# Hybrid attention and retention layer: program order for the first four gate products, and later stores of scaled attention pieces

## The chip, the cores and the metric

One core of one Trainium2 chip runs the whole layer in one launch. The metric is the device time of that launch in microseconds, the median of several executions. Lower is better. Engines are named as in the profile: PE is TensorE's matmul, PEld its weight load, DVE is VectorE, ACT is ScalarE, POOL is GpSimd, SP is SyncE, which here only issues DMAs.

## The reference

One layer over 1024 latent tokens of width 1024, with 256 context tokens as a prefix. After a modulated RMSNorm one projection feeds neighbourhood attention, bidirectional retention and two merge gates. The part that this case touches:

```
(xq, xk, xv, xrq, xrk, xrv, xrg, xga, xgb) = split(hx @ w_in)
o_na  = neighbourhood_attention(xq, xk, xv, context keys)
o_ret = norm(bi_retention(xrq, xrk, xrv)) * silu(xrg)
merged = sigmoid(xga) * (o_na @ w_proj_na) + sigmoid(xgb) * (o_ret @ w_proj_ret)
x = x + g1 * (merged @ w_out)
x = x + g2 * conv_ffn(modulate(rmsnorm(x)))
```

All of it is in float32. The output is a final RMSNorm of `x`.

## The kernel before, in words

**Arithmetic.** A float32 product is made of three matmuls on split operands: high times high, high times low, low times high. `split` (L88, L89) makes the halves: ScalarE casts a tile to its high half (L88), VectorE subtracts it from the source to get the low half (L89). Weight tiles in split form are `wc` (six buffers, shared by all stages); as they come from memory they are `raw` (three buffers) or, in the gate stage, `wr` (ten buffers).

**Stages, in order of time.** Start and norm, attention, retention (four heads, some 390 to 720 us), the projection of attention (`pn`), the gate products (class `Gates`, some 770 to 930 us), the projection of retention with the merge (`pr`), the output projection (`om`), the conv FFN (`u` again, with another class on the same base `Seven`), and its down projection (`y`).

**The gate products.** `Seven` makes a product of 2 by 2 blocks with seven block products in place of eight. For one gate, a11, a12, a21 and a22 are blocks of the weights and B11 to B22 blocks of the activations. s1 to s4 are sums of weight blocks (L1423 to L1426, on POOL, but for the first gate, where VectorE makes s1 to s3), T1 to T4 are sums of activations made earlier (`hx_sums`, tiles `hxT`). `step(n)` issues block product n, 12 matmuls at L1409 into one of three PSUM banks X, Y, Z (`u`):

- step 0: a11 times B11 into X; ScalarE copies X to p1 (`pu`, L1449)
- step 1: s2 times T2 into Y; VectorE makes u2 = Y + p1 (`pu`, L1452)
- step 2: s1 times T1 into Z
- step 3: s3 times T3 on top of Y; VectorE makes u3 = Y + p1 (`pu`, L1458), and the first result block
- steps 4 to 6: a12 on top of X, a22 on top of Y, s4 on top of Z; three more result blocks

Step 3 writes the bank that u2 reads, so it follows u2. `interleaved` overlaps the gates: the second gate's step 0 comes behind the first gate's step 3, then the two alternate. In program order that is gate and step (0,0), (0,1), (0,2), (0,3), (1,0), (0,4), (1,1), (0,5), (1,2), (0,6), (1,3). Each `prod` splits its own weights right before its matmuls, except the first gate's a11, which `wload` splits during the `pn` stage (`first`).

**What sets the order.** The kernel is written in program order, and a scheduler of the framework then orders the instructions of each engine. An instruction wrapped in `late` (L533) keeps its place in program order on its engine. Each engine, and SP's queue of DMA issues, runs strictly in the order that results; a waiting instruction holds up all behind it.

**The scaled pieces.** `scaled` (L1265) runs during retention, one step per call of `next(rows)`. Each of 32 steps loads a 128 by 128 piece of attention sums (`os`, from `d_sum`) and the matching reciprocals (`or`, from `d_rec`), multiplies on VectorE (L1283, pinned with `late`), and stores the piece to `d_on` (L1274). The load runs one step ahead; the store is issued one step behind its multiply; both tiles have three buffers. All these DMAs are issued on SP, in one queue with the retention weights (`raw`, L93), the stores and loads of `down_sums` (`d_w`, `pj`), and others. The retention weights end in tiles `wc` or, for the last two of a head, `wx`.

Of the kernel before, what the change touches and what calls it, by code (L numbers as in the profile page):

```python
# [8 lines left out]
F32 = mybir.dt.float32  # L9
F32R = mybir.dt.float32r  # L10
AF = mybir.ActivationFunctionType
ALU = mybir.AluOpType
# [4 lines left out]
P = 128  # L17
D = 1024
KB = D // P
# [21 lines left out]
def tile_hybrid_layer(ctx, tc: tile.TileContext, io, dbg=None):  # L41
    nc = tc.nc
    vec, act, pool, pe, sync = nc.vector, nc.scalar, nc.gpsimd, nc.tensor, nc.sync
# [43 lines left out]
    def split(hi, lo, src, lo_eng=None):  # L87
        act.copy(hi, src)  # L88
        (lo_eng or vec).tensor_tensor(lo, src, hi.bitcast(F32), ALU.subtract)  # L89
# [221 lines left out]
    first = [[wtile() for _ in range(2)] for _ in range(3)]  # L311
# [221 lines left out]
    late = tc.keep_in_program_order  # L533
# [47 lines left out]
    nraw, nxt = {}, {}  # L581
# [472 lines left out]
    rt = sb("ret", "right")  # L1054
# [209 lines left out]

    def scaled():  # L1265
        def load(pr, j):
            o, r = (rt.tile([P, P], F32, tag=t, bufs=3, name=t) for t in ("os", "or"))
            sync.dma_start(o, d_sum[pr, :, j])
            src = d_rec[2 * pr : 2 * pr + 2, j * P : (j + 1) * P].unsqueeze(1).to_broadcast([2, HD, P])
            sync.dma_start(r, src)  # L1270
            return o, r

        def store(pr, j, o):
            sync.dma_start(d_on[pr, :, :, j].rearrange("h p q -> p h q"), o.rearrange("p (h q) -> p h q", h=2))  # L1274

        steps = [(pr, j) for pr in range(NPAIR) for j in range(NJ)]
        nxt, done = load(*steps[0]), None
        yield
        for n, at in enumerate(steps):
            o, r = nxt  # L1280
            if n + 1 < len(steps):
                nxt = load(*steps[n + 1])
            late(vec.tensor_tensor(o, o, r, ALU.mult))  # L1283
            if done:
                store(*done)
            done = (*at, o)
            yield
        store(*done)

    rows = scaled()  # L1290

# [30 lines left out]
    mix, last = None, (None, None)  # L1322
    for h in range(RH):
        head = Head(h)
        for i in range(NCB + NTB):
# [3 lines left out]
            last = (head, i)  # L1329
# [38 lines left out]
    def g_ps(name):  # L1368
        return pg.tile([P, 512], F32, tag="g", bufs=6, name=name)
# [44 lines left out]
        tc.add_manual_dep(ins.ins, prev.name, mybir.DependencyInfo(mybir.DependencyClass.Sync, mybir.DependencyReason.DATA))  # L1414

    class Seven:
        loaded, first = False, None

        def load(self, pin=lambda ins: ins, eng=None):
            self.loaded, own, eng = True, late if eng else lambda ins: ins, eng or pool  # L1420
# [7 lines left out]
        def fetch(self, b, half):  # L1428
            pass

        def prod(self, bank, a, c, first, last, w=None):
            if w is None:
                w = wtile()
                split(w[:, 0], w[:, 1], a)
            for k, (xh, xl) in enumerate(self.moving(c)):
                open3(bank, w[:, 0, k * P : (k + 1) * P], w[:, 1, k * P : (k + 1) * P], xh, xl, first and k == 0, last and k == KH - 1)

# [4 lines left out]
        def step(self, n):  # L1442
            if n == 0:
                if not self.loaded:
                    self.load()
                self.banks()
                self.p1, self.u2, self.u3 = (self.tmp() for _ in range(3))
                self.prod(self.X, self.a11, "B11", True, False, self.first)
                act.copy(self.p1, self.X)  # L1449
            elif n == 1:  # L1450
                self.prod(self.Y, self.s2, "T2", True, False)
                vec.tensor_tensor(self.u2, self.Y, self.p1, ALU.add)  # L1452
            elif n == 2:
                self.prod(self.Z, self.s1, "T1", True, False)
            elif n == 3:
                self.fetch(1, 1)
                self.prod(self.Y, self.s3, "T3", False, False)
                vec.tensor_tensor(self.u3, self.Y, self.p1, ALU.add)  # L1458
                self.add(1, 1, self.Z, self.u3)
            elif n == 4:  # L1460
                self.fetch(0, 0)
                self.prod(self.X, self.a12, "B21", False, True)
                self.c11()
            elif n == 5:
                self.fetch(1, 0)
                self.prod(self.Y, self.a22, "T4", False, True)
                self.add(1, 0, self.Y, self.p1)
            else:
                self.fetch(0, 1)
                self.prod(self.Z, self.s4, "B22", False, True)  # L1470
                self.add(0, 1, self.Z, self.u2)

    HALVES = {"B11": (0, 0), "B21": (KH, 0), "B22": (KH, 1)}
# [4 lines left out]
    class Gates(Seven):  # L1478


        def __init__(self, kind, n):
            self.kind, self.n = kind, n
            w = io["w_rg" if kind == "ret" else "w_gate"]
            self.src = {(b, i): w[n, b, i] for b in range(2) for i in range(2)}
            self.c = {}
# [42 lines left out]
    for db in range(KB):  # L1528
        if db + 2 < KB:
            wp[db + 2] = [wload(io["w_pna"][db + 2, 0])]  # L1530
        if db in HX_SUMS:
            hs = hx_sums(HX_SUMS.index(db))
            next(hs)
        for half in range(2):
            sl_ = slice(half * 512, half * 512 + 512)
            m = g_ps("pn")
            mm_a(m, wp[db], lambda k: ona[0][:, k, sl_], lambda k: ona[1][:, k, sl_])
            t = onap.tile([P, 512], F32, tag="pn", bufs=3, name="pnt")
            if (db, 0) in spilled:
                g = onap.tile([P, 512], F32, tag="sg", bufs=2, name="sgt")  # L1540
                sync.dma_start(g, d_gate[2 * db, half])
                act.activation(g, g, AF.Sigmoid)
                vec.tensor_tensor(t, m, g, ALU.mult)
            else:
                act.copy(t, m)
            act.dma_start(d_pn[db, half], t)
        if db == HX_SUMS[-1]:
            gu[0].first = wload(gu[0].src[0, 0])
            gu[0].load(late, vec)
        if db in HX_SUMS:  # L1550
            next(hs)
# [24 lines left out]
    steps = interleaved(0, len(gu))  # L1576
    n0, fetched, wp0 = steps.index((len(gu) - 1, 0)), None, []
    fetches = {d: (k // 8, k % 8) for k, d in enumerate((-6, -5, -4, -3, 1, 2, 3, 4, 7, 9))}
    for n, (i, k) in enumerate(steps):
        gu[i].step(k)  # L1580
        if n % 3 == 1:
            next(gate_sums, None)
        if fetched:
            split(*fetched[0], fetched[1])
            fetched = None
        if n - n0 in fetches:
            fetched = orr_raw(*fetches[n - n0])
        if n >= len(steps) - 3 and len(wp0) < 2:
            wp0.append(wload(io["w_pret"][0, len(wp0)]))
# [237 lines left out]
    class Up(Seven):  # L1827


        def __init__(self, n, j):  # L1830
            self.n, self.j = n, j
            self.src = {(b, i): io["w_up"][j, b, i] for b in range(2) for i in range(2)}

        def raw(self, src):
# [293 lines left out]
```

## Time and profile before

| what | before |
|---|---|
| median of 3 runs | 1764.5 us (1763.49 to 1765.6) |
| profiled execution: device time | 1764.47 us |
| profiled execution: span in the trace | 1762.7 us |
| mean granted TensorE clock | 0.992 |
| instructions | 24593 |
| moved by DMA | 268.20 MB, mean 152 GB/s |

In the rows below a number pair at the start is start and length in us from the span's start, then engine, line, operation, output and input tiles, shape, and how many in a row; a bracket at the end is idle time just before, with what ended it. `ACTq` and `SPq` are DMA issues on those engines' queues. The rows of the stretches give busy time and instruction counts of PE, PEld, DVE, ACT and POOL, then the granted TensorE clock (1.00 is full), the busy share of the DMA engines and GB/s. The rows of waits give total us, times and the longest.

### The profile page before, as it was taken

Reading aid. Unit: us, or ns where it says so; the run is one execution under the profiler, and the core shown is the slowest. Engines: PE = TensorE matmul, PEld = TensorE weight load, DVE = VectorE, ACT = ScalarE, POOL = GpSimd, SP = SyncE. Lnnn points to the kernel's source line nnn. Section 1 sums busy time; section 2 is a strip of 40 time slices with the busy share of each in tenths; the row PEclk is TensorE's granted clock in tenths of the full one; section 3 lists DMA queues with packets and bytes.
Section 4 is the critical chain, followed back from the end, with each engine's and each line's share of the span. In section 5 each row is a group of like instructions: output and inputs, shape, how many; then the busy total and the mean of one; then the engine's idle time right before and its main releaser. Section 6 shows DMA issues by size and latency. Waiting matters only on the chain.

```text
span 1762.7 us, 24593 instructions
## 1 busy us (share of the span) xinstructions
PE 1715.2 (97%) x8262; PEld 1415.7 (80%) x8262; DVE 1317.0 (75%) x2509; ACT 848.1 (48%) x1802; POOL 550.6 (31%) x458
## 2 busy tenths in 40 slices
PE   8799999999999999999999999999999999999997
PEld 3588888888788888878888888888888888888886
DVE  5978888765687777777665556888899899876655
ACT  5666666652443434543444333544444444554444
POOL 2610000002233343136422400265555555111444
PEclk9899999999999999999999999999999999999998
DMA  9134334533333312567659643733323332586754
GB/s 348 52 116 135 105 113 120 154 127 105 94 111 87 109 57 77 188 218 246 209 176 314 227 144 130 259 127 111 99 90 99 118 113 90 179 287 193 244 167 150
DMA packets 157247, 268.20 MB, mean 152 GB/s; under 512 B 25184, under 2 KB 45888, under 8 KB 157120
## 3 DMA queue, kind: packets, MB, share of 16 engines
q1 hardware_dynamic: 139200, 245.65, 42.9%
q10 hardware_dynamic: 17920, 20.98, 3.3%
q8 instruction: 65, 1.06, 0.3%
q14 instruction: 62, 0.51, 0.1%
HBM read 192.32 MB, written 71.61 MB: 150 GB/s over the span
## 4 chain that ended last, share of the span: by engine, by line
PE 45%; issue 5%; DVE 3%; POOL 3%; ACT 1%; DMA 0%; POOLq 0%; ACTq 0%; DVEq 0%
PE u L1409 27%; PE y L1409 4%; PE om L123 2%; PE om L124 2%; PE om L125 2%; PE pr L113 2%; PE pr L112 2%; PE pr L114 2%; DVE wc L89 1%; PE u L113 1%; PE u L114 1%; PE u L112 1%; POOL x L1942 1%; PE pn L113 0%; PE pn L112 0%
## 5 line engine op out<-in xcount | busy, mean ns | idle before, releaser
L1409 PE MATMUL u<-T,wc 128*128 128x512 f32 x960 | 225.5, 390 | 0.3 <-ACT pu L1449 0.2
L1409 PE MATMUL y<-wc,ahl 128*128 128x512 f32 x924 | 212.2, 391 | 2.3 <-DVE wc L89 1.8
L1409 PEld LDWEIGHTS u<-T,wc 128*128 128x128 f32 x960 | 179.4, 188 | 40.9 <-ACT pu L1449 3.6
L1409 PEld LDWEIGHTS y<-wc,ahl 128*128 128x128 f32 x924 | 174.4, 189 | 39.8 <-DVE wc L89 2.5
L89 DVE TENSOR_TENSOR wc<-ur,wc 128x512 fp32r<-128x512 f32 x137 | 126.2, 923 | 62.3 <-ACT wc L88 62.3
L88 ACT CAST wc<-ur 128x512 fp32r<-128x512 f32 x137 | 85.1, 622 | 125.1 <-PE y L1409 72.6
L113 PE MATMUL mm<-low,wc 128*128 128x512 f32 (+1 forms) x328 | 124.4, 379 | 0.0
L1409 PE MATMUL u<-h2a,wc 128*128 128x512 f32 x480 | 112.5, 390 | 0.7 <-DVE pu L1458 0.7
L112 PE MATMUL mm<-hx,wc 128*128 128x512 f32 x264 | 106.9, 405 | 0.3 <-DVE vc L223 0.3
L1409 PEld LDWEIGHTS u<-h2a,wc 128*128 128x128 f32 x480 | 89.9, 188 | 20.1 <-DVE pu L1458 1.1
L114 PE MATMUL mm<-hx,wc 128*128 128x512 f32 x264 | 105.9, 401 | 0.0
L1409 PE MATMUL u<-hxT,wc 128*128 128x512 f32 x384 | 92.5, 397 | 3.9 <-DVE pu L1452 3.9
L88 ACT CAST wc<-s 128x512 fp32r<-128x512 f32 x80 | 49.6, 621 | 90.2 <-PE u L1409 87.0
L125 PE MATMUL mm<-wc,low 128*128 128x512 f32 (+1 forms) x240 | 91.4, 381 | 0.0
L1409 PEld LDWEIGHTS u<-hxT,wc 128*128 128x128 f32 x384 | 73.5, 192 | 19.9 <-issue 4.3
L89 DVE TENSOR_TENSOR wc<-s,wc 128x512 fp32r<-128x512 f32 x80 | 85.8, 1072 | 3.1 <-ACT wc L88 2.6
L1552 POOL TENSOR_TENSOR col<-col,bcol 128x32 f32<-128x32 f32 x1 | 0.2, 250 | 278.4 <-DVE st L482 278.4
L88 ACT CAST wc<-raw 128x512 fp32r<-128x512 f32 x93 | 57.3, 620 | 47.8 <-DMA raw<-in_w_ret 7.1
L89 DVE TENSOR_TENSOR wc<-raw,wc 128x512 fp32r<-128x512 f32 x93 | 63.3, 689 | 18.6 <-ACT wc L88 18.2
L123 PE MATMUL mm<-wc,hx 128*128 128x512 f32 x192 | 75.2, 392 | 0.6 <-ACT r L1111 0.6
L124 PE MATMUL mm<-wc,hx 128*128 128x512 f32 x192 | 75.2, 392 | 0.0
L89 DVE TENSOR_TENSOR wc<-wr,wc 128x512 fp32r<-128x512 f32 x55 | 53.4, 976 | 18.2 <-ACT wc L88 17.5
(396 smaller groups left out, 4663.1 us busy)
## 6 DMA issues: line engine op xcount, KB each, us to landing
ur<-in_w_up SPq DMA_DIRECT2D x80, 256.0 KB
ur<-d_a SPq DMA_DIRECT2D x77, 256.0 KB
aw<-in_w_ada SPq DMA_DIRECT2D x32, 512.0 KB
pj<-in_w_down SPq DMA_DIRECT2D x44, 256.0 KB
d_w<-pj SPq DMA_DIRECT2D x44, 256.0 KB
d_a<-sa SPq DMA_DIRECT2D x44, 256.0 KB
ur<-d_w SPq DMA_DIRECT2D x44, 256.0 KB
d_a<-at SPq DMA_DIRECT2D x33, 256.0 KB
```

Of the source, the lines that this page charges most:

```text
L88: act.copy(hi, src)
L89: (lo_eng or vec).tensor_tensor(lo, src, hi.bitcast(F32), ALU.subtract)
L112: pe.matmul(out, wh, xh, start=k == 0, stop=False)
L113: pe.matmul(out, wh, xl, start=False, stop=False)
L114: pe.matmul(out, wl, xh, start=False, stop=k == n - 1)
L123: pe.matmul(out, ah, bh, start=first, stop=False)
L124: pe.matmul(out, ah, bl, start=False, stop=False)
L125: pe.matmul(out, al, bh, start=False, stop=last)
L1409: pe.matmul(out, a, b, start=first and n == 0, stop=last and n == 2, skip_group_check=True)
L1552: pool.tensor_tensor(col[:, 16:48], col[:, 16:48], bcol[:, 16:48], ALU.add)
L1942: pool.tensor_tensor(z, z, fg[:, gs(dh)], ALU.mult)
```

## The change

Four edits, none of which adds or removes arithmetic.

1. The weight split of `Seven` becomes a method `split(n)`, kept by the number of the step in a table `w`; `prod` splits only what is not in the table. The first gate's s2 and s1 are split during the `pn` stage, in front of its last half, and pinned there. s3 of the first gate is split behind step 0, a11 of the second gate behind step 1 (which also loads the second gate there), a12 of the first gate behind step 2, all pinned.
2. In the first four products, the copy p1 (ScalarE), u2 and u3 (VectorE) are pinned too.
3. In `scaled`, the store is issued two steps behind its multiply.
4. In `scaled`, `os` has four buffers and `or` two.

```diff
@@ scaled
-            o, r = (rt.tile([P, P], F32, tag=t, bufs=3, name=t) for t in ("os", "or"))
+            o, r = (rt.tile([P, P], F32, tag=t, bufs=n, name=t) for t, n in (("os", 4), ("or", 2)))
...
             late(vec.tensor_tensor(o, o, r, ALU.mult))
-            if done:
-                store(*done)
-            done = (*at, o)
+            done.append((*at, o))
+            if n > 1:
+                store(*done.pop(0))
             yield
-        store(*done)
+        for d in done:
+            store(*d)
@@ Seven
-        loaded, first = False, None
+        loaded, pin = False, staticmethod(lambda ins: ins)
...
-        def prod(self, bank, a, c, first, last, w=None):
-            if w is None:
-                w = wtile()
-                split(w[:, 0], w[:, 1], a)
+        def split(self, n, pin=lambda ins: ins):
+            a = (self.a11, self.s2, self.s1, self.s3, self.a12, self.a22, self.s4)[n]
+            self.w[n] = w = wtile()
+            pin(act.copy(w[:, 0], a))
+            pin(vec.tensor_tensor(w[:, 1], a, w[:, 0].bitcast(F32), ALU.subtract))
+
+        def prod(self, bank, n, c, first, last):
+            if n not in self.w:
+                self.split(n)
+            w = self.w.pop(n)
...
-                act.copy(self.p1, self.X)
+                self.pin(act.copy(self.p1, self.X))
...
-                vec.tensor_tensor(self.u2, self.Y, self.p1, ALU.add)
+                self.pin(vec.tensor_tensor(self.u2, self.Y, self.p1, ALU.add))
...
-                vec.tensor_tensor(self.u3, self.Y, self.p1, ALU.add)
+                self.pin(vec.tensor_tensor(self.u3, self.Y, self.p1, ALU.add))
@@ pn stage, ahead of each half of a block
+            if (db, half) == (KB - 1, 1):
+                for n in (1, 2):
+                    gu[0].split(n, late)
...
-            gu[0].first = wload(gu[0].src[0, 0])
+            gu[0].w[0] = wload(gu[0].src[0, 0])
@@ gate stage
+    ahead = {0: (0, 3), 1: (1, 0), 2: (0, 4)}
     for n, (i, k) in enumerate(steps):
+        gu[i].pin = late if n < 4 else lambda ins: ins
         gu[i].step(k)
+        if n in ahead:
+            j, k = ahead[n]
+            if not gu[j].loaded:
+                gu[j].load()
+            gu[j].split(k, late)
```

What becomes of it on the engines, at three places. PE and POOL have the same order before and after.

ScalarE, at the end of the `pn` stage and the start of the gates, before. `wr_8924`, `wr_8923` and `wr_8925` are the first gate's s2, s1 and s3, `wr_8921` its a12, `wr_9070` and `wr_9075` the second gate's a11 and s2, and `pu_8988` is p1:

```order
L88 CAST wc_9004<-wr_8924 128x512
L88 CAST wc_9028<-wr_8923 128x512
L1545 COPY pnt_8968<-pn_8955 128x512
L1559 COPY arow_8977<-tpa_8975 32x128
L1546 DMA d_pn_64<-pnt_8968 128x512
L88 CAST wc_9045<-wr_8925 128x512
L88 CAST wc_9088<-wr_9070 128x512
L1449 COPY pu_8988<-u_8985 128x512
L88 CAST wc_9109<-wr_8921 128x512
L88 CAST wc_9128<-wr_9075 128x512
```

The same place with the change, where the lines are those of the new file, `wr_9030` and `wr_9035` are the second gate's a11 and s2, and `pu_8994` is p1:

```order
L1435 CAST wc_8955<-wr_8924 128x512
L1435 CAST wc_8958<-wr_8923 128x512
L1555 COPY pnt_8974<-pn_8961 128x512
L1569 COPY arow_8983<-tpa_8981 32x128
L1556 DMA d_pn_64<-pnt_8974 128x512
L1456 COPY pu_8994<-u_8991 128x512
L1435 CAST wc_9010<-wr_8925 128x512
L1435 CAST wc_9042<-wr_9030 128x512
L1435 CAST wc_9065<-wr_8921 128x512
L1435 CAST wc_9128<-wr_9035 128x512
```

p1 has moved ahead of the casts of s3 and of the second gate's a11; the rest stands as it did.

VectorE at the same time, before; `pu_8989` is u2 and `pu_8990` is u3, `wr_8917` is the first gate's a22 and `wr_9074` the second gate's s1:

```order
L89 TENSOR_TENSOR wc_9004<-wr_8924,wc_9004 128x512
L89 TENSOR_TENSOR wc_9028<-wr_8923,wc_9028 128x512
L89 TENSOR_TENSOR wc_9045<-wr_8925,wc_9045 128x512
L89 TENSOR_TENSOR wc_9088<-wr_9070,wc_9088 128x512
L89 TENSOR_TENSOR wc_9109<-wr_8921,wc_9109 128x512
L89 TENSOR_TENSOR wc_9128<-wr_9075,wc_9128 128x512
L1452 TENSOR_TENSOR pu_8989<-u_8986,pu_8988 128x512
L89 TENSOR_TENSOR wc_9146<-wr_8917,wc_9146 128x512
L89 TENSOR_TENSOR wc_9170<-wr_9074,wc_9170 128x512
L1458 TENSOR_TENSOR pu_8990<-u_8986,pu_8988 128x512
```

And with the change, where `pu_8995` is u2:

```order
L1436 TENSOR_TENSOR wc_8955<-wr_8924,wc_8955 128x512
L1436 TENSOR_TENSOR wc_8958<-wr_8923,wc_8958 128x512
L1436 TENSOR_TENSOR wc_9010<-wr_8925,wc_9010 128x512
L1459 TENSOR_TENSOR pu_8995<-u_8992,pu_8994 128x512
L1436 TENSOR_TENSOR wc_9042<-wr_9030,wc_9042 128x512
L1436 TENSOR_TENSOR wc_9065<-wr_8921,wc_9065 128x512
L1436 TENSOR_TENSOR wc_9128<-wr_9035,wc_9128 128x512
L1436 TENSOR_TENSOR wc_9146<-wr_8917,wc_9146 128x512
L1436 TENSOR_TENSOR wc_9170<-wr_9034,wc_9170 128x512
L1465 TENSOR_TENSOR pu_8996<-u_8992,pu_8994 128x512
```

u2 has moved ahead of three low halves, of the second gate's a11, the first gate's a12 and the second gate's s2; u3 has kept its place.

SP's queue at the first change of head in retention, before; `raw_5013` and `raw_5018` are the last two weight tiles of a head, `raw_5970` on are the next head's, `os_4912` and `os_4976` are the second and third piece:

```order
L93 DMA raw_5013<-in_w_ret 128x512
L1274 DMA d_on_59<-os_4912 128x2x64
L1270 DMA or_5143<-d_rec_58 128x1x128
L93 DMA raw_5018<-in_w_ret 128x512
L93 DMA raw_5970<-in_w_ret 128x512
L1268 DMA os_5142<-d_sum_57 128x128
L1274 DMA d_on_59<-os_4976 128x2x64
L1270 DMA or_5235<-d_rec_58 128x1x128
L93 DMA raw_5975<-in_w_ret 128x512
```

And with the change, where the last two tiles are `raw_5012` and `raw_5017`:

```order
L93 DMA raw_5012<-in_w_ret 128x512
L1270 DMA or_5069<-d_rec_58 128x1x128
L1274 DMA d_on_59<-os_4912 128x2x64
L93 DMA raw_5017<-in_w_ret 128x512
L93 DMA raw_5969<-in_w_ret 128x512
L93 DMA raw_5974<-in_w_ret 128x512
L1270 DMA or_5142<-d_rec_58 128x1x128
L1268 DMA os_5233<-d_sum_57 128x128
L1274 DMA d_on_59<-os_4976 128x2x64
```

The store and the load of reciprocals have changed places, the loads belong to earlier pieces than before, and one of the next head's weight loads stands one piece further forward.

More of the change, by code (lines that the diff above doesn't have):

```diff
@@ L1276, in scaled @@
         steps = [(pr, j) for pr in range(NPAIR) for j in range(NJ)]
-        nxt, done = load(*steps[0]), None
+        nxt, done = load(*steps[0]), []
         yield
@@ L1447, in step @@
                 self.p1, self.u2, self.u3 = (self.tmp() for _ in range(3))
-                self.prod(self.X, self.a11, "B11", True, False, self.first)
-                act.copy(self.p1, self.X)
+                self.prod(self.X, 0, "B11", True, False)
+                self.pin(act.copy(self.p1, self.X))
             elif n == 1:
-                self.prod(self.Y, self.s2, "T2", True, False)
-                vec.tensor_tensor(self.u2, self.Y, self.p1, ALU.add)
+                self.prod(self.Y, 1, "T2", True, False)
+                self.pin(vec.tensor_tensor(self.u2, self.Y, self.p1, ALU.add))
             elif n == 2:
-                self.prod(self.Z, self.s1, "T1", True, False)
+                self.prod(self.Z, 2, "T1", True, False)
             elif n == 3:
                 self.fetch(1, 1)
-                self.prod(self.Y, self.s3, "T3", False, False)
-                vec.tensor_tensor(self.u3, self.Y, self.p1, ALU.add)
+                self.prod(self.Y, 3, "T3", False, False)
+                self.pin(vec.tensor_tensor(self.u3, self.Y, self.p1, ALU.add))
                 self.add(1, 1, self.Z, self.u3)
@@ L1461, in step @@
                 self.fetch(0, 0)
-                self.prod(self.X, self.a12, "B21", False, True)
+                self.prod(self.X, 4, "B21", False, True)
                 self.c11()
@@ L1465, in step @@
                 self.fetch(1, 0)
-                self.prod(self.Y, self.a22, "T4", False, True)
+                self.prod(self.Y, 5, "T4", False, True)
                 self.add(1, 0, self.Y, self.p1)
@@ L1469, in step @@
                 self.fetch(0, 1)
-                self.prod(self.Z, self.s4, "B22", False, True)
+                self.prod(self.Z, 6, "B22", False, True)
                 self.add(0, 1, self.Z, self.u2)
@@ L1481, in __init__ @@
         def __init__(self, kind, n):
-            self.kind, self.n = kind, n
+            self.kind, self.n, self.w = kind, n, {}
             w = io["w_rg" if kind == "ret" else "w_gate"]
@@ L1830, in __init__ @@
         def __init__(self, n, j):
-            self.n, self.j = n, j
+            self.n, self.j, self.w = n, j, {}
             self.src = {(b, i): io["w_up"][j, b, i] for b in range(2) for i in range(2)}
```

## The prediction

> **What bounds the kernel now.** I read the page's busy shares first, then TensorE's timeline for every idle stretch, then the granted clock around the longest one inside the gates, then the chain that ended last there, and last the queues of ScalarE, VectorE and SyncE at the lines that the change touches.
>
> ```profile
> PE 1715.2 (97%) x8262; PEld 1415.7 (80%) x8262; DVE 1317.0 (75%) x2509; ACT 848.1 (48%) x1802; POOL 550.6 (31%) x458
> ```
>
> TensorE (PE) is the bound. The other engines matter only where they make it wait, so a change that adds and removes no arithmetic can win at most those waits. The timeline of PE at the start of the gate products:
>
> ```profile
> 772.95 5.71 PE L1409 MATMUL u<-hxT,wc 128*128 128x512 f32 x24
> 782.54 5.42 PE L1409 MATMUL u<-hxT,wc 128*128 128x512 f32 x12 [3.88 <-DVE pu L1452]
> 787.80 0.40 PE L1409 MATMUL u<-hx,wc 128*128 128x512 f32 x1
> ...
> 793.30 8.32 PE L1409 MATMUL u<-hxT,wc 128*128 128x512 f32 x36
> ```
>
> I number the products in program order: 0 to 3 are the first gate's, 4 is the second gate's first (a11), 5 the first gate's with a12, 6 the second gate's with s2. Each is 12 matmuls. The 24 from 772.95 are products 1 and 2 (into banks Y and Z). The 12 from 782.54 are product 3, which accumulates into Y and therefore waits for u2 (`pu`, L1452), which reads Y. That wait is 3.88 us. The second loss is in the same rows. At full pace 36 matmuls take 8.32 us, so one starts each (8.32 - 0.39) / 35 = 0.2266 us and 12 need 2.72 us. Product 3's twelve take 787.80 - 782.54 = 5.26 us. The stretches with busy times and, behind them, granted clock, DMA share and GB/s say why:
>
> ```profile
> 773.00:778.70 5.70, 5.67 (x25) 4.19 (x23) 2.30 (x5) 1.63 (x4) 4.71 (x3) 1.00 0.99 338
> 778.70:782.50 3.80, 0.00 (x0) 0.00 (x0) 3.67 (x4) 1.66 (x3) 3.72 (x3) 0.80 0.70 261
> 782.50:788.00 5.50, 5.46 (x13) 4.32 (x14) 2.65 (x2) 0.00 (x0) 4.98 (x4) 0.52 0.36 101
> 788.00:793.00 5.00, 5.00 (x23) 4.09 (x22) 3.33 (x5) 3.64 (x5) 0.01 (x1) 1.00 0.98 287
> ```
>
> The granted clock falls to 0.80 inside the idle stretch, stands at 0.52 for the 5.5 us behind it, and is back at 1.00 from 788. The idle costs its own length and then about as much again in slow matmuls.
>
> The chain that ended last, ahead of that product:
>
> ```profile
> 771.55 4.80 DMA wr<-in_w_rg
> 776.60 0.48 POOL wr L1423
> ...
> 777.98 1.60 POOL wr L1424
> 779.61 0.63 ACT wc L88
> 780.26 1.54 DVE wc L89
> 781.80 0.61 DVE pu L1452
> 782.54 146.92 PE u L1409 x636
> ```
>
> None of this belongs to u2. The weights that land, are summed on POOL and split on ACT and DVE are those of the second gate. u2 needs only bank Y and p1, yet stands behind them on VectorE, and p1 stands behind one of them on ScalarE:
>
> ```profile
> 772.38 0.62 ACT L88 CAST wc<-wr 128x512 fp32r<-128x512 f32 x1 [0.25 <-ACT arow L1559]
> 777.04 0.62 ACT L88 CAST wc<-wr 128x512 fp32r<-128x512 f32 x1 [4.04 <-DMA wr<-in_w_rg]
> 777.57 0.58 ACT L1449 COPY pu<-u 128x512 f32<-128x512 f32 x1
> ...
> 772.65 1.89 DVE L89 TENSOR_TENSOR wc<-wr,wc 128x512 fp32r<-128x512 f32 x3
> 777.69 0.76 DVE L89 TENSOR_TENSOR wc<-wr,wc 128x512 fp32r<-128x512 f32 x1 [3.16 <-ACT wc L88]
> 778.70 3.10 DVE L89 TENSOR_TENSOR wc<-wr,wc 128x512 fp32r<-128x512 f32 x2 [0.25 <-PE u L1409]
> 781.72 0.68 DVE L1452 TENSOR_TENSOR pu<-u,pu 128x512 f32<-128x512 f32 x1
> 782.32 2.83 DVE L89 TENSOR_TENSOR wc<-wr,wc 128x512 fp32r<-128x512 f32 x2
> ```
>
> **Part 1: order of the first four gate products.** On both engines it is a move of one row; PE and POOL keep their orders. ScalarE does p1 ahead of the casts of s3 and of the second gate's a11. VectorE does u2 right behind the low half of s3.
>
> Step by step on the clock of before. Product 0's last matmul starts 0.23 ahead of 772.95 and takes 0.39, so it ends about 773.1, and p1 runs 773.15 to 773.7. Now p1 is ahead of the s3 cast, which before ran at 772.38; that cast waits for p1 and runs 773.7 to 774.3, and its low half 774.35 to 775.05. Product 1 ends near half of the 5.71 us, about 776.0, and u2 (0.68 us) ends at 776.75. Product 3 needs s3's low half (775.05), u2 (776.75), and PE free of products 1 and 2: last start 772.95 + 5.71 - 0.39 = 778.27, next 0.23 later, **778.50**. PE is the last of the three by 1.75 us, so the wait is gone, not shortened. With no idle there is no slow stretch: product 3 takes 2.72 us and product 4 starts at 781.22 instead of 787.80. **Gain 6.58 us**: 4.04 of later start (3.88 idle, the rest the tail of the last matmul) and 2.54 of slow clock.
>
> [...]
>
> What is late next: product 4 needs the second gate's a11, ready at 777.69 + 0.76 = 778.45, wanted at 781.22 (2.8 us to spare). Product 5 wants a12 at 783.94; it stands in the 3.10 us group that ends at 781.8. The second gate's s2 for product 6 is in that group too and is wanted at 786.66 (4.9 us to spare). The two low halves of 2.83 us end by 785.2 and are wanted from 789.38. Behind p1 on ScalarE stands only the s3 cast, whose reader now has 778.50 - 775.05 = 3.4 us. The splits of s1 and s2 written earlier in the code keep their places in both queues, since VectorE's 772.65 row is fed in order by earlier work; cost and gain 0. The earlier call that loads the second gate moves no row of SP or POOL: 0.
>
> Does the gain last? The chain runs on PE without a break for 146.92 us and 636 matmuls. Work that does not follow PE must still be in time 6.6 us earlier:
>
> ```profile
> 787.21 1.93 SPq L1490 DMA_DIRECT2D wr<-in_w_rg  x4
> 792.99 1.29 POOL L1423 TENSOR_TENSOR wr<-wr 128x512 f32<-128x512 f32 x1 [5.35 <-DMA wr<-in_w_rg]
> 805.98 1.28 POOL L1423 TENSOR_TENSOR wr<-wr 128x512 f32<-128x512 f32 x1 [3.65 <-DVE wc L89]
> ...
> 806.90 0.39 PE L1409 MATMUL u<-hx,wc 128*128 128x512 f32 x1
> ```
>
> The third gate's weights are landed by 792.99 and its first product starts at 806.90, which becomes 800.3: 7 us left. From the fourth gate on (POOL at 805.98) the weights wait for a VectorE split ahead of them, which follows PE. I carry the whole 6.58.
>
> **Part 2: scaled pieces.** `scaled` runs inside retention. The arithmetic, the bytes and VectorE's order stay; SyncE's order changes. The rows that show whether PE feels it, at the first change of head, between the multiply's group and two rows of the waits:
>
> ```profile
> L1283 DVE TENSOR_TENSOR os<-os,or x32: 277/651/751, 441.4 to 680.7; 128x128 f32<-128x128 f32 x32
> ...
> 450.17 0.74 DVE L1283 TENSOR_TENSOR os<-os,or 128x128 f32<-128x128 f32 x1
> ...
> 453.44 0.28 DVE L1283 TENSOR_TENSOR os<-os,or 128x128 f32<-128x128 f32 x1
> ...
> 450.94 0.38 SPq L1274 DMA_DIRECT2D d_on<-os  x1
> 451.37 0.51 SPq L1270 DMA_DIRECT2D or<-d_rec  x1
> 451.97 0.88 SPq L93 DMA_DIRECT2D raw<-in_w_ret  x2
> ...
> 456.23 0.62 ACT L88 CAST wx<-raw 128x512 fp32r<-128x512 f32 x1 [1.66 <-DMA raw<-in_w_ret]
> ...
> 456.90 0.44 PE L123 MATMUL mm<-wx,hc 128*128 128x384 f32 x1 [1.53 <-ACT wx L88]
> ...
> 440.00:480.00 40.00, 36.86 (x192) 31.12 (x191) 27.18 (x87) 16.24 (x44) 9.38 (x14) 1.00 0.31 87
> ...
> PE mm L123 <- ACT wx L88: 4.1, 3, 1.5
> ...
> SPq L1274 <- DVE os L1283: 128.9, 28, 7.2
> ```
>
> There are 32 multiplies, the first at 441.4. Today the store waits for the multiply that ends at 450.91; behind it on SP stand the `or` load (0.51 us) and the weight load whose landing 4.2 us later makes PE wait 1.53 us. In the new order the store is two steps old and waits for nothing, but `or` has two buffers instead of three, so its load must wait for the previous step's multiply: the same multiply at 450.91, with the same two issues (0.38 and 0.51) between it and the weight load at 451.97. The wait changes its owner, not its end. The weight loads that do move forward (one place ahead of an `or` and an `os`) are the next head's and nobody waits for them. New risk on VectorE: the multiply waits for an `or` issued later. The load is issued after the multiply two steps back, so that of 453.44 can be loaded from 442 on, some 11 us ahead, with the closest pair of steps between; a landing takes 4 to 5 us in the rows above. Bounds: at best all three waits of this kind go, -4.1; at worst both issues, 0.38 + 0.51, come on top at each of three heads, +2.7. I take 0, the end that the row at 450.94 is next to.
>
> **Sum.** The profiled execution took 1764.47 us around its span of 1762.7, and the median is 1764.5, so it speaks for the median. 1764.5 - 6.58 + 0 = **1757.9 us**, 0.37% less.
>
> **The rivals.**
> A. A shorter wait replaces the long one: a11 or s2 of the second gate lands or is summed later than now, because its transfer shares a DMA share of 0.99 (773.0 to 778.7). It decides from 2.8 us of delay on (a11) or 4.9 (s2). Against it: no transfer moves there. A wait of 1 to 3 us, with or without a slow clock after it, leaves 1759 to 1762.
> B. The gain is taken back later. In the conv stage VectorE is near its own limit:
>
> ```profile
> 1200.00:1300.00 100.00, 99.98 (x440) 82.20 (x440) 91.77 (x90) 44.64 (x63) 57.66 (x33) 1.00 0.33 106
> ```
>
> PE is still at 99.98 of 100 there, and VectorE's work starts from PE's banks, so it shifts along; 1761.5 to 1765 if it did not.
> C. Slower: the wait at each change of head grows from 1.53 us to the 3.88 us that the gates show, from which the clock falls. The mechanism is SP: if the new `or` wait holds back the weight load by another 2.35 us, PE idles 2.35 more and pays 2.54 of slow clock, at three heads 14.7. That gives 1764.5 - 6.6 + 14.7 = 1772.6. [...] For it: SP waits 28 times for this multiply today. Against it: the same multiply, the same issues.
> D. It does not do what it says: product 3 waited for something else that u2 only hid. The chain shows none; s3's low half was done at 774.5. 1764.5.
>
> **Chances.** Forecast 0.77 (its own range 1755.5 to 1760.0), A 0.10, B 0.07, C 0.03, D 0.03. Faster by over 0.2% (3.5 us, about what a measurement here tells from no change): the forecast and half of A, 0.82. Within 0.2%: half of A, most of B, and D, 0.14. Slower: C and a little of B, 0.04. The range reaches from 2.9 us under the forecast, most of part 2's best case, to 1761.5, which takes in part 2's worst case and most of A.
>
> **What would show it.** Right: no idle stretch ahead of product 3, granted clock 1.00 from 773 to 793 on the shifted clock, u2 directly behind s3's low half on VectorE, `pu` on ScalarE some 4 us earlier; the three `wx` waits still near 4.1 us in sum, with SyncE's waits for L1283 now at the `or` load; every later stage 6.6 us earlier. Wrong: a wait at product 4 or later with a11 or s2 behind it, `wx` waits above 2 us each, or stages behind 930 us that shift by less.

## The result, and the profile after

| what | before | after |
|---|---|---|
| median, side by side on one chip, 12 runs each | 1766.57 us (1762.48 to 1774.86) | 1757.53 us (1754.85 to 1764.18) |
| profiled execution: device time | 1764.47 us | 1756.5 us |
| profiled execution: span | 1762.7 us | 1754.7 us |
| mean granted TensorE clock | 0.992 | 0.993 |
| instructions | 24593 | 24598 |

The ratio is 0.9947 with a 95% interval of 0.993 to 0.9964: of 1766.57 us that is 9.4 us less, between 6.4 and 12.4. The forecast was 1757.9 us and 6.6 us less. Executions of one kernel differ by some 10 us, so most of what follows is read from stages of the traces and not from medians. Ratios below are to before as measured beside the run, and leave out two executions at a low mean clock: 1828.42 us at 0.888 (u2 behind s2) and 2127.03 us at 0.752 (`or` as two DMAs).

**The gates.** PE's timeline of the kernel after, from the end of product 0:

```profile
768.25 0.48 PE L1410 MATMUL u<-hx,wc 128*128 128x512 f32 x1
...
771.08 8.32 PE L1410 MATMUL u<-hxT,wc 128*128 128x512 f32 x36
779.24 0.39 PE L1410 MATMUL u<-hx,wc 128*128 128x512 f32 x1
```

Products 1, 2 and 3 are one row of 36 matmuls in 8.32 us, where before there were 24, an idle of 3.88 us and 12 slow ones. Product 4 follows at 779.24. The stretches of the same time, with the granted clock third from the end:

```profile
770.00:773.00 3.00, 3.00 (x15) 2.49 (x14) 1.95 (x4) 1.11 (x2) 2.92 (x2) 1.00 0.84 307
773.00:778.70 5.70, 5.70 (x27) 4.73 (x26) 4.62 (x5) 2.81 (x5) 5.52 (x4) 1.00 1.01 375
778.70:790.00 11.30, 11.30 (x52) 9.35 (x51) 10.13 (x10) 4.85 (x8) 7.87 (x6) 1.00 0.76 242
```

PE is busy all the time at a clock of 1.00, with a DMA share as high as before (1.01 against 0.99). ScalarE and VectorE, from their timelines:

```profile
771.28 0.59 ACT L1456 COPY pu<-u 128x512 f32<-128x512 f32 x1 [1.71 <-PE u L1410]
771.76 0.62 ACT L1435 CAST wc<-wr 128x512 fp32r<-128x512 f32 x1
```

```profile
772.41 0.69 DVE L1436 TENSOR_TENSOR wc<-wr,wc 128x512 fp32r<-128x512 f32 x1 [1.05 <-ACT wc L1435]
774.00 0.69 DVE L1459 TENSOR_TENSOR pu<-u,pu 128x512 f32<-128x512 f32 x1 [0.89 <-PE u L1410]
774.88 8.12 DVE L1436 TENSOR_TENSOR wc<-wr,wc 128x512 fp32r<-128x512 f32 x5 [0.19 <-ACT wc L1435]
```

p1 starts at once behind product 0, u2 behind product 1 (its idle is ended by PE, no longer by weights), and the low halves of the second gate run behind it, where nobody waits for them.

**The changes of head.** Waits of PE and of SP's queue in the kernel after:

```profile
PE mm L123 <- ACT wx L88: 2.0, 3, 0.7
```

```profile
SPq L1270 <- DVE os L1283: 86.6, 26, 5.8
SPq L1268 <- DMA d_on<-os: 43.0, 24, 2.6
```

SP waits at the `or` load (L1270) for the multiply, as forecast. But PE's three waits for `wx` fell from 4.1 to 2.0 us, which was not. The first change of head, SP's, VectorE's and ScalarE's rows:

```profile
451.84 0.51 SPq L1270 DMA_DIRECT2D or<-d_rec  x1
452.40 0.47 SPq L1274 DMA_DIRECT2D d_on<-os  x1
452.96 1.38 SPq L93 DMA_DIRECT2D raw<-in_w_ret  x3
```

```profile
451.06 0.75 DVE L1283 TENSOR_TENSOR os<-os,or 128x128 f32<-128x128 f32 x1
```

```profile
456.31 0.62 ACT L88 CAST wx<-raw 128x512 fp32r<-128x512 f32 x1 [0.86 <-DMA raw<-in_w_ret]
```

The order was store, `or`, weight load, and is now `or`, store, weight load. I call them the old and the new order. From the weight load's issue to its cast it was 456.23 - 451.97 = 4.26 us, and is now 456.31 - 452.96 = 3.35.

**Where the 8.0 us of span came from.** Two marks of PE before (the first wait of retention and product 0), then the first of them after:

```profile
394.61 0.50 PE L123 MATMUL mm<-wc,hx 128*128 128x512 f32 x1 [0.63 <-ACT r L1111]
770.12 0.48 PE L1409 MATMUL u<-hx,wc 128*128 128x512 f32 x1
```

```profile
395.77 0.50 PE L123 MATMUL mm<-wc,hx 128*128 128x512 f32 x1 [0.63 <-ACT r L1111]
```

Start to first wait: 1.16 us more, in code that the change doesn't touch. First wait to product 0: 375.51 to 372.48, **3.03 less** (part 2's stage). Product 0 to product 4: 17.68 (787.80 - 770.12) to 10.99, **6.69 less** (part 1). All that follows together: 0.56 more. Sum 1.16 - 3.03 - 6.69 + 0.56 = -8.00.

### The profile page after: what moved, and what is told of

Same layout as the page of the kernel before. It is cut to its first block, busy times and chain, and to the rows that moved or that the text cites. A ratio compares the mean times of both kernels' runs of the same rounds, so it can differ in the third digit from the quotient of the medians.

```text
span 1754.7 us, 24598 instructions
## 1 busy us (share of the span) xinstructions
PE 1712.0 (98%) x8262; PEld 1414.3 (81%) x8262; DVE 1321.8 (75%) x2509; ACT 846.7 (48%) x1802; POOL 547.5 (31%) x458
## 3 DMA queue, kind: packets, MB, share of 16 engines
q8 instruction: 65, 1.06, 0.3%
## 4 chain that ended last, share of the span: by engine, by line
PE 43%; issue 6%; DVE 4%; POOL 3%; DMA 2%; ACT 1%; SPq 0%; POOLq 0%; DVEq 0%; ACTq 0%
PE u L1410 28%; PE y L1410 4%; PE pr L112 2%; PE pr L114 2%; PE pr L113 2%; PE om L125 1%; PE om L123 1%; PE om L124 1%; PE pn L113 1%; PE pn L112 1%; PE pn L114 1%; DMA vo<-d_h 1%; POOL x L1959 1%; DVE wc L1436 0%; DVE T L89 0%
## 5 line engine op out<-in xcount | busy, mean ns | idle before, releaser
L89 DVE TENSOR_TENSOR wc<-ur,wc 128x512 fp32r<-128x512 f32 x77 | 60.9, 794 | 60.5 <-ACT wc L88 60.5
L88 ACT CAST wc<-ur 128x512 fp32r<-128x512 f32 x77 | 47.6, 620 | 76.4 <-PE y L1410 71.4
L1436 DVE TENSOR_TENSOR wc<-wr,wc 128x512 fp32r<-128x512 f32 x55 | 56.3, 1031 | 16.1 <-ACT wc L1435 15.9
```

Of the source, the lines that this page charges most:

```text
L1436: pin(vec.tensor_tensor(w[:, 1], a, w[:, 0].bitcast(F32), ALU.subtract))
```

## The experiments

Open was why the `wx` waits halved, and whether the gates' gain is part 1 alone. Two theories for the waits: **A**, the `or` load holds up the weight load behind it, because it reads two rows of reciprocals spread to 64 partitions each, and comes in slowly; **B**, the order itself, or the store that stood ahead of both, lengthened the landing.

### Each part alone

The gates alone (edits 3 and 4 undone), in the kernel after:

```diff
-(("os", 4), ("or", 2))      # buffers
+(("os", 3), ("or", 3))
-            if n > 1:
-                store(*done.pop(0))
+            if done:
+                store(*done)
```

> The gate part alone, with the scaled pieces as before. Theory 1, both parts pay: no idle stretch ahead of product 3, gates 6.4 to 6.6 us shorter, the three wx waits still near 4.1 us, ratio to before about 0.9963 (6.5 of 1764.5). Rival, the gate part pays for all and the shorter wx waits are chance: ratio about 0.995 and wx waits anywhere from 2 to 4 us.

And the scaled pieces alone, in the kernel before (the same lines the other way round):

> The scaled part alone, with the gates as before. Theory 1: the wx waits fall from 4.1 to about 2.0 us, the weight load behind the load of reciprocals lands some 3.5 us after its issue instead of 4.3, the time from the first head to the projection is about 3 us shorter, ratio about 0.998; the idle stretch of 3.9 us in the gates stays. Rival, chance: wx waits near 4 us and ratio 1.000.

Measured: 1763.77 us for the gates alone, ratio 0.9981 (0.9962 to 1.0001), and 1764.25 us for the pieces alone, ratio 0.9981 (0.9961 to 1.0002). By the medians neither part is told from nothing. Their stages say more. The gates alone take 11.09 us from product 0 to product 4, no idle. The pieces alone keep the idle, in PE's timeline:

```profile
781.32 5.06 PE L1410 MATMUL u<-hxT,wc 128*128 128x512 f32 x12 [4.39 <-DVE pu L1453]
```

and have 1.8 us of `wx` waits. So each part does its own work, and the gates are part 1's alone. One reason why the gates alone can stay short of 6.6 us shows in their profiled execution, at the first and the second change of head. PE's rows, with three short idles at the first and a long one at the second:

```profile
448.29 0.44 PE L123 MATMUL mm<-wc,hc 128*128 128x384 f32 x1 [0.42 <-ACT wc L88]
449.01 0.46 PE L124 MATMUL mm<-wc,hc 128*128 128x384 f32 x1 [0.28 <-DVE wc L89]
450.36 0.41 PE L123 MATMUL mm<-wc,hc 128*128 128x384 f32 x1 [0.54 <-DVE r L1120]
...
534.76 0.44 PE L123 MATMUL mm<-wx,hc 128*128 128x384 f32 x1 [1.75 <-ACT wx L88]
```

The stretches behind them:

```profile
450.00:456.00 6.00, 5.43 (x25) 5.13 (x25) 4.07 (x10) 1.94 (x6) 1.46 (x2) 0.72 0.59 147
...
536.00:540.00 4.00, 4.00 (x16) 4.00 (x15) 2.02 (x6) 2.18 (x8) 1.42 (x2) 0.57 0.29 99
```

In this execution the clock fell at two changes of head (means of 0.72 and 0.57 in these stretches), behind three idles of at most 0.54 us and behind one of 1.75 us, and its retention took 377.7 us where before, with the same order of SP, took 375.5. Whether the other eleven executions lost time in the same way is not shown.

### How much idle brings the slow clock

u2 put back, still pinned, behind the low halves of the second gate's a11, the first gate's a12 and the second gate's s2:

```diff
-    ahead = {0: (0, 3), 1: (1, 0), 2: (0, 4)}
+    ahead = {0: [(0, 3)], 1: [(1, 0)], 2: [(0, 4), (1, 1)]}
...
+            if n == 2:
+                gu[0].make_u2()
```

> The changed kernel with u2 put back behind the low half of the second gate's s2 on VectorE, p1 left early. PE should idle about 2.2 us ahead of product 3, since the sum for s2 comes from GpSimd at about 775.7 and its low half and u2 take until 778.7, where PE is free at 776.5. [...] Rival, slow matmuls follow any idle in proportion: product 3 takes about 4.1 us and the loss is 3.6 us.

Measured: 1764.51 us, ratio 0.998 (0.9959 to 1.0). PE's and VectorE's rows:

```profile
781.19 4.20 PE L1410 MATMUL u<-hxT,wc 128*128 128x512 f32 x12 [3.71 <-DVE pu L1450]
```

```profile
775.42 5.03 DVE L1436 TENSOR_TENSOR wc<-wr,wc 128x512 fp32r<-128x512 f32 x3 [1.40 <-ACT wc L1435]
780.37 0.68 DVE L1450 TENSOR_TENSOR pu<-u,pu 128x512 f32<-128x512 f32 x1
```

The idle is back at 3.71 us with p1 early: u2's place on VectorE alone makes it. It is longer than I had expected, because the three low halves took 5.03 / 3 = 1.68 us each at this place, and one alone 0.69 (772.41 above). So this run does not say what an idle of 2 us does. Product 3 takes 785.19 - 781.19 = 4.00 us, which is 1.28 us above full pace. Then the same with one low half less ahead of u2 (s2 stays behind it):

> The kernel after, with u2 put back behind one low half less than in the run before this one: behind the second gate's a11 and the first gate's a12. There three low halves took 5.03 us from 775.42, and u2 ran at 780.37 with 3.71 us of idle ahead of product 3; one of them less makes u2 end near 779.4 and the idle 2.0 us (1.5 to 2.5). From product 0's first matmul to product 4's it was 10.99 us in after, 16.14 with 3.71 idle, 17.7 with 3.88. If an idle of 2 us leaves the granted clock at 1.00, it is 13.0 here; if the clock falls after any idle, 14 or more.

Measured: 1765.14 us (one run). PE's timeline and the stretch behind the idle:

```profile
780.87 4.58 PE L1410 MATMUL u<-hxT,wc 128*128 128x512 f32 x12 [1.93 <-DVE pu L1450]
785.29 0.39 PE L1410 MATMUL u<-hx,wc 128*128 128x512 f32 x1
```

```profile
781.00:783.00 2.00, 2.00 (x6) 1.56 (x7) 2.00 (x2) 0.00 (x0) 1.93 (x2) 0.58 0.19 57
```

The idle is the 2.0 us expected, and the clock falls all the same, to 0.58: product 3 takes 785.29 - 780.87 = 4.42 us where 2.72 is full pace, 1.70 us lost. From product 0 to product 4 it is 14.78 us against 10.99 in after. Half the idle of before brings two thirds of its slow part (2.54), and more than the 3.71 us of the run ahead (1.28): the length of the idle does not set the size.

### What the `or` load does to the weight load

Each `or` load as two DMAs of 64 rows, in the kernel after:

```diff
-            sync.dma_start(r, src)
+            for h in range(2):
+                sync.dma_start(r[h * HD : (h + 1) * HD], d_rec[2 * pr + h : 2 * pr + h + 1, j * P : (j + 1) * P].to_broadcast([HD, P]))
```

> The changed kernel with each load of reciprocals cut in two loads of 64 rows, so that its slowest dimension is 64 and not 2. Theory A, the load of reciprocals runs on few DMA engines and the weight load behind it waits for those: the weight load lands in about 3 us, wx waits fall from 2.0 to under 1.0 us in sum, 1 us faster than the changed kernel. Rival B, what counts is how many issues stand between the multiply and the weight load on SyncE: one more issue of about 0.5 us, wx waits rise to about 3 us, 1 us slower than the changed kernel.

Measured: 1760.33 us, ratio 0.9957 (0.9936 to 0.9978), `wx` waits 1.8 us. The first change of head, on SP:

```profile
451.28 1.09 SPq L1270 DMA_DIRECT2D or<-d_rec  x2
452.46 0.54 SPq L93 DMA_DIRECT2D raw<-in_w_ret  x1
453.05 0.43 SPq L1274 DMA_DIRECT2D d_on<-os  x1
```

The scheduler put the store behind the weight load. The weight load's cast came 3.64 and 3.61 us after its issue at the first two heads (in after 3.35 and 3.67), and the second `or` issue costs SP some 0.5 us ahead of it. Both forecasts miss: A wanted a landing in 3 us and waits under 1.0 us, B waits of about 3. Cutting the load in two, with 64 rows as its outermost dimension, did not make it a quick one: a half lands 2.5 us after its issue in the median, a whole plain load, as tried further below, in 1.8 to 2.2. In the next run the store is taken off SP (after, `sync.dma_start(d_on...)` becomes `act.dma_start(d_on...)`), so that one `or` load stands right ahead of the weight load:

> The kernel after, with the stores of the scaled pieces issued by ScalarE's DMA queue instead of SyncE's: on SyncE the weight load then follows the `or` load directly and is issued about 0.6 us after the start of the `or` issue instead of 1.12. Theory A (the weight load lands when the `or` load lets it): the landing counted from the start of the `or` issue stays at 4.2 to 4.9 us, so issue to cast grows to about 4.0, and the three wx waits stay near 2.0 us in sum. Theory B (the store ahead of the `or` load is what lengthens the landing): issue to cast stays at 3.1 to 3.8 and each wx wait falls by about 0.5, to 0.5 us in sum; product 0 then starts 371 us after the first wait at 395 us instead of 372.5. ScalarE gets 32 more issues of about 0.4 us, which cost at most the waits of TensorE for casts, under 1 us.

Measured: 1760.57 us, ratio 0.9958 (0.9943 to 0.9974), `wx` waits 3.6 us. SP's and ScalarE's rows:

```profile
451.82 0.51 SPq L1270 DMA_DIRECT2D or<-d_rec  x1
452.44 1.51 SPq L93 DMA_DIRECT2D raw<-in_w_ret  x3
```

```profile
457.29 0.62 ACT L88 CAST wx<-raw 128x512 fp32r<-128x512 f32 x1 [3.85 <-DMA raw<-in_w_ret]
```

No store stands ahead on SP, the weight load goes out 0.5 us sooner, and lands later: 4.85, 3.79 and 4.56 us after its issue at the three heads. B's form with the store falls. A expected about 4.0; it is A's side, with more than A's size, and A's 2.0 us of `wx` waits missed too. Then the form of the `or` load itself, in the kernel before, with the old order:

```diff
-            src = d_rec[2 * pr : 2 * pr + 2, j * P : (j + 1) * P].unsqueeze(1).to_broadcast([2, HD, P])
-            sync.dma_start(r, src)
+            sync.dma_start(r, d_sum[pr, :, (j + 1) % NJ])
```

> The kernel before, with the `or` load alone changed: it reads a plain 128x128 piece of the stored sums instead of the reciprocals spread over 64 rows each, so the scaling by the right reciprocal is left out; count, order and size of the DMA issues stay (store, `or`, weight load). In the two traces with this order so far the last weight load of a head is cast 4.1 to 4.8 us after its issue; in the two with the order `or`, store, weight load 3.1 to 3.8 us. Theory A (the spread `or` load, whose rows trickle in, stands ahead of the weight load in the DMA engines): 3.0 to 3.7 us here, and PE's three waits for wx fall from 4.1 us to under 2. Theory B (the store ahead of both, or the order itself, makes the difference): 4.1 to 4.8 us and about 4 us of wx waits, as before.

Measured: 1760.83 us (one run). The weight load was cast 2.65, 3.56 and 3.19 us after its issue, and the `wx` waits are 0.5 us in sum. The old order is not slow by itself. How the load comes in shows in stretches of 0.8 us from the weight load's issue, GB/s last; before:

```profile
451.97:452.77 0.80, 0.80 (x6) 0.80 (x5) 0.80 (x3) 0.59 (x3) 0.14 (x1) 1.00 0.25 56
452.77:453.57 0.80, 0.80 (x7) 0.80 (x6) 0.80 (x3) 0.00 (x0) 0.60 (x1) 1.00 1.53 79
453.57:454.37 0.80, 0.80 (x8) 0.80 (x6) 0.15 (x1) 0.17 (x1) 0.00 (x0) 1.00 0.19 60
```

With the plain `or` load:

```profile
450.30:451.10 0.80, 0.80 (x6) 0.80 (x6) 0.80 (x3) 0.63 (x3) 0.10 (x1) 1.00 0.36 85
451.10:451.90 0.80, 0.80 (x7) 0.80 (x6) 0.80 (x3) 0.00 (x0) 0.65 (x1) 1.00 0.92 186
451.90:452.70 0.80, 0.80 (x8) 0.80 (x6) 0.20 (x1) 0.16 (x1) 0.00 (x0) 1.00 0.84 269
```

In the first 2.4 us from the weight load's issue, behind the spread load (56 + 79 + 60) x 0.8 = 156 KB move in all, behind the plain one (85 + 186 + 269) x 0.8 = 432 KB. The sizes asked for are the same: 64 KB for `or`, 256 KB for each weight load.

### A third `or` buffer

In the kernel after, `or` with three buffers (and 7 in place of 8 for `pj`, to make room):

> The kernel after, with three buffers for `or` again (four for `os` stay; to make room the sums of the down weights in the same pool have 7 buffers instead of 8). No issue of SyncE waits for the running multiply any more: the wait of the `or` load for it, 86.6 us in sum, falls under 30. Theory (the weight load is late because it stands behind an issue that waits for the multiply): it is issued 1 us or more earlier, the wx waits fall from 2.0 to under 0.7 us, and product 0 starts 371 us or less after the first wait at 395 us: 1 to 2 us less than after. Rival (the weight load itself waits for a buffer that a cast frees at about the same time): wx waits about 2.0, time as after.

Measured: 1758.72 us, ratio 0.9957 (0.9944 to 0.9971), `wx` waits 2.0 us, 372.1 us to product 0. SP's waits:

```profile
SPq L1270 <- DVE os L1283: 78.3, 23, 4.8
```

The wait that I expected to fall under 30 us stays at 78.3. I read it so: SP has nothing else to do and runs ahead as far as the buffers allow, so its next issue stands on some multiply with two buffers or with three. The theory behind this run falls. The stage's 372.1 us also show that having two `or` buffers is not what brought the 3.0 us.

### The reciprocals spread once

A correct form of the plain load: eight transfers from DRAM to DRAM early in retention spread the reciprocals, and the 32 `or` loads read plain pieces. In the kernel after:

```diff
+    d_rx = [dram.tile([NJ, 2, HD, P], F32, name=f"d_rx{n}") for n in range(NPAIR)]
...
-            src = d_rec[2 * pr : 2 * pr + 2, j * P : (j + 1) * P].unsqueeze(1).to_broadcast([2, HD, P])
-            sync.dma_start(r, src)
+            sync.dma_start(r, d_rx[pr][j].rearrange("h r q -> (h r) q"))
...
+        def spread(pr):
+            for h in range(2):
+                src = d_rec[2 * pr + h].rearrange("(j q) -> j q", j=NJ).unsqueeze(0).to_broadcast([HD, NJ, P])
+                sync.dma_start(d_rx[pr][:, h].rearrange("j r q -> r j q"), src)
```

> The kernel after, with the reciprocals spread to 64 rows once, by eight transfers from DRAM to DRAM early in retention, so that each of the 32 `or` loads reads a plain 128x128 piece; count, size and place of the `or` loads stay. From the first wait (L123 for r, near 395 us) to product 0 it is 375.5 and 377.7 us with the order store, `or`, weight load, 372.1 to 373.3 with the order `or`, store, weight load, and 369.3 in the run whose `or` loads are plain pieces (old order). Theory A (the spread `or` load costs, and all that stands behind it in the DMA engines pays): 368.5 to 370 here too, the wx waits under 1 us, the time 3 us less than the kernel after: about 1754. Rival (part 2 and the plain load gain separately): 366 to 367 and about 1751. Rival (the eight transfers move 2 MB in the stretch after 394 and are paid back there): 371 or more, no gain over after.

The same lines in the kernel before:

> The kernel before, with the same plain `or` loads (the reciprocals spread once by eight transfers) and nothing else: product 3 keeps its idle of 3.9 to 4.4 us and the slow clock. Theory A: from the first wait to product 0 369 to 370 us as in the run above it, so that the order of store and `or` load is worth nothing once the `or` load is plain; the time about 6 us under before. Rival (the order is worth 3 us whatever the load): 372 to 373 here, against 369 to 370 above.

And after once more, on the same chip:

> The kernel after unchanged, beside the two runs above on the same chip: 372 to 373.3 us from the first wait to product 0, 10.99 us from product 0 to product 4 with no idle, wx waits of about 2 us in sum, and 6 to 12 us under before.

Measured: 1756.17 us with after's order, ratio 0.9934 (0.9911 to 0.9957); 1759.43 us with before's, 0.9949 (0.9929 to 0.997); after itself 1758.29 us, 0.9942 (0.9922 to 0.9963). First wait and product 0, with after's order and then with before's:

```profile
393.80 0.50 PE L124 MATMUL mm<-wc,hx 128*128 128x512 f32 x1 [0.63 <-ACT r L1112]
763.12 0.48 PE L1418 MATMUL u<-hx,wc 128*128 128x512 f32 x1
```

```profile
395.53 0.50 PE L124 MATMUL mm<-wc,hx 128*128 128x512 f32 x1 [0.63 <-ACT r L1112]
764.90 0.48 PE L1417 MATMUL u<-hx,wc 128*128 128x512 f32 x1
```

369.32 and 369.37 us: with plain `or` loads the order is worth nothing. All profiles, read from the same marks:

| kernel | order on SP | `or` load | first wait to product 0, us | product 0 to product 4, us |
|---|---|---|---|---|
| before | old | spread | 375.5 | 17.7 |
| gates alone | old | spread | 377.7 | 11.1 |
| after | new | spread | 372.5 | 11.0 |
| after again | new | spread | 372.4 | 11.0 |
| pieces alone | new | spread | 372.6 | 18.3 |
| three `or` buffers | new | spread | 372.1 | 11.0 |
| u2 behind s2 / behind a12 | new | spread | 372.1 / 373.3 | 16.1 / 14.8 |
| store on ScalarE's queue | no store | spread | 375.0 | 11.2 |
| `or` as two DMAs | store behind the weight load | halves | 372.8 | 11.0 |
| plain pieces, before | old | plain | 369.3 | 17.7 |
| spread once, before | old | plain | 369.4 | 17.6 |
| spread once, after | new | plain | 369.3 | 11.0 |

Each row is one profile. Three of the retention stages hold stretches at half clock: the gates alone two of 3.41 us each, u2 behind a12 and the store on ScalarE's queue one each. The kernel with both is the fastest by its trace (span 1752.6 us); its 2.1 us under after by the medians lie inside the intervals.

## Why the prediction was right, and where it was not

**Part 1, the idle and its removal: right, shown.** The idle follows u2's place on VectorE: there in every kernel that has u2 behind the second gate's weights, gone in the seven that have not. Product 4 was forecast 781.22 - 770.12 = 11.10 us behind product 0 and comes 10.99 behind it; the gain was 6.58 and is 6.69.

**The slow clock: right in kind, and not of one size.** In the three other kernels of the table that kept before's gates it cost, above 2.72 us for product 3, about 2.2 us (2.17 with the pieces alone: 786.21 - 781.32 - 2.72), 2.54 in before, 1.70 behind an idle of 1.93, 1.28 behind one of 3.71. What sets the size shows when the stretches are laid on the steps of the clock, in before and with u2 behind a12:

```profile
780.97:787.79 6.82, 5.25 (x12) 4.13 (x13) 4.18 (x4) 0.29 (x1) 6.43 (x5) 0.50 0.32 92
```

```profile
781.31:784.72 3.41, 3.41 (x10) 2.63 (x9) 3.41 (x3) 0.00 (x0) 3.25 (x3) 0.50 0.27 90
```

The clock is 0.50 for 6.82 us in before and for 3.41 us there, and 1.00 on both sides. Product 3 loses half of the time that it spends in such a stretch: (787.79 - 782.54) / 2 = 2.6 us in before, where 2.54 was measured, and 3.41 / 2 = 1.7 in the other, where 1.70 was. So the 2.54 in the sum is the size of one execution. The steps keep a grid: the traces' records of the clock, which the views don't print, hold eleven changes in before and eleven in after, in each trace whole multiples of 3.413 us apart, and counted from the span's start the two grids are 1.95 us out of step. So where a step falls is not fixed by the place in the kernel. Nor was PE idle for a whole step ahead of the slow stretches: in the 3.42 us ahead of before's (777.55 to 780.97) it was busy for 1.11 us, with u2 behind a12 for 1.48 of 3.41 (777.90 to 781.31), in the gates alone for 2.17 (447.40 to 450.81).

**What is late next, and whether the gain lasts: right.** PE has no wait between 770 and 790, the transfers at a DMA share of 1.01 are in time (rival A), and of the gain 0.4 us is lost between product 4 and the conv stage (370.54 us before, 370.94 after) and 0.2 in the conv stage itself (372.64 and 372.84 to the first matmul of the down projection; rival B). The second profile of after does lose time at the start of the conv stage, as told at the end; so does a kernel with before's gates (the plain pieces).

**Part 2, taken as 0: the step that was wrong; it is -3.0.** "The wait changes its owner, not its end" holds for the issue: the weight load goes out 1.06 us after the multiply's end before (451.97 - 450.91) and 1.15 after (452.96 - 451.06 - 0.75). What I left out is the landing. I took "whose landing 4.2 us later" as the weight load's own time. It is the time of what stands ahead of it: 0.6 us behind a spread `or` load the weight load is cast 4.1 to 4.8 us after its issue (before and the gates alone, six heads), 1.1 us behind it, with the store between, 3.1 to 3.8 us (after and the pieces alone, six heads). The new order doesn't take work away; it starts the slow load 0.4 us sooner after the multiply and puts the store's issue where the weight load would only have queued. The runs with plain loads show the whole size, 375.5 - 369.4 = 6.1 us, of which the change wins half. My bound of -4.1 held it, but I chose the other end for the reason that the row was near, when it spoke of the issue alone.

That the time hangs on the spread load is shown: with plain loads the order is worth nothing. How that load holds up the others is shown in part. The traces keep each DMA packet and each update of a semaphore, which the views don't print. In after, at the first head, the `or` load ends in two completion writes of 4 bytes (454.78 and 454.79; the two updates of its semaphore come at 455.10 and 455.18). Of the store behind it 14 come at 453.62 to 453.76; I take the two at 455.01 and 455.02 for its last, since its semaphore has 14 updates by 454.12 and two more at 455.34 and 455.36. The `or` load's 128 packets of 512 bytes go mostly two at a time and take 453.14 to 454.77, 1.63 us; the 128 of a plain `os` piece in the same trace take 467.59 to 468.13, 0.54 us. In before, 14 packets of the weight load, begun at 453.03 to 453.32, take 1.14 to 1.97 us each, where later ones take 0.084; this is the DMA share of 1.53 at 79 GB/s.

The number of completion writes is not the whole reason, though. Each half in the run with two DMAs ends in 16 completion writes, and the 128 packets still go mostly two or three at a time: 452.52 to 453.92, 1.40 us. What the halves share with the spread load, and the plain pieces do not, is that one row of 512 bytes is read 64 times. No run separates this from the rest, for instance a load of 128 different rows with an outermost dimension of 2.

**Rival C asked for too long an idle.** It had the wait grow to the 3.88 us of the gates before the clock falls. The clock fell behind 1.75 us (gates alone) and 2.12 us (store on ScalarE's queue) at a change of head, and stayed at 1.00 behind 1.53 us (before) and 1.54 us (gates alone). It also fell behind three idles of at most 0.54 us (gates alone) and of 0.56 us (u2 behind a12), and not behind two of 0.28 and 0.56 us at the same place in before. So no single length parts the idles with a slow clock behind them from those without. Its place was well seen, though: in the gates alone the clock fell at two changes of head.

**The time itself** came out 0.4 us from the forecast by luck, because two misses cancel: by the medians the gain was 9.0 us and not 6.6, and before's median beside it was 1766.57 us and not 1764.5.

**Open:** why the landing counted from the start of the `or` issue is still some 0.4 us shorter in the new order (4.47 us after, 4.86 before, at the first head), and why the store on ScalarE's queue makes it longer than either there (5.47 us; at the second head it is 4.40, and 4.74 in before). Open too is what exactly brings a step of the clock down.

## What to carry to other kernels

When a wait for a DMA is weighed, ask what is ahead of it in the DMA queue and in what form, not only when it is issued: a small load that spreads few rows over many partitions can cost those behind it more than its own bytes (here 6.1 us of retention, with loads of 64 KB). Where an engine is held by a small operation, look what it stands behind; if none of that is its input, program order is worth more than a scheduler's guess (here 6.69 us). SP's queue, which prefetches, stood at the limit of its buffers with two and with three for `or` (86.6 and 78.3 us of waits): a buffer more need not remove such a wait.

## What had not been expected of the hardware

The clock of TensorE falls after much less idle than in the gates of before: after 1.75 us of idle at a change of head, 1.93 in the gates, and twice after three idles of at most 0.56 us within 3 us. It falls for 3.41 us (u2 behind a12) or 6.82 (before), and not each time, so it is one source of scatter between executions of one kernel. An example is the second profile of after, PE's row at the start of the conv stage and the stretch behind it:

```profile
1153.28 7.11 PE L1410 MATMUL u<-T,wc 128*128 128x512 f32 x23 [2.60 <-ACT pu L1456]
```

```profile
1153.30:1158.00 4.70, 4.70 (x14) 3.75 (x15) 3.78 (x6) 0.53 (x2) 2.00 (x1) 0.64 0.43 148
```

The first profile of the same program has 0.3 us at this place and a clock of 1.00. The 2.60 us wait with the slow clock behind it is there in seven of the thirteen profiles, with either order, and the second span of after is 1.8 us longer (1756.5 us) although its retention and its gates take as long as the first's. A low half on VectorE takes 0.69 us by itself and 1.68 in the row of three (5.03 us), in a stretch in which POOL adds the weights; why was not tried.
